# Fused two-block transformer on one core: mixer outputs transposed in steps of their own, and the second layer's transfers moved behind the ninth weights of the first feed-forward

## The chip, the cores and the metric

The kernel runs on one core of a Trainium2 chip. The metric is the device time of one execution in microseconds (us). The program is one launch: TensorE (PE) multiplies, VectorE (DVE) and ScalarE (ACT) read its results and prepare operands, GpSimd (POOL) does a few small operations, and SyncE (SP) issues the transfers from HBM.

## The reference

A first block (retention and RWKV mixers and 16 experts) is followed by a second block of two layers. Only the second block is touched. It works on 256 tokens of 1024 features in fp32:

```
for layer in range(2):
    z = rmsnorm(x, norm_mix[layer]) @ w_in[layer]
    o_a, o_b, o_c, o_d = nsa_mixer(...), diff_mixer(...), mlstm_mixer(...), dilated_mixer(...)
    x = x + concatenate([o_a, o_b, o_c, o_d], axis=-1) @ w_out[layer]
    h = rmsnorm(x, norm_ffn[layer])
    x = x + (silu(h @ w_gate[layer]) * (h @ w_up[layer])) @ w_down[layer]
return rmsnorm(x, norm_final)
```

Each mixer gives 256 of the 1024 columns that `w_out` multiplies. The inner width of the feed-forward is 2816, which the kernel takes in 11 strips of 256.

## The kernel before

**Tiles.** The 256 tokens are two tiles of 128 (index `i`). A matmul of fp32 operands is made of three passes: each operand is split into a rounded part (`hi`, `wh`) and what is left (`lo`, `wl`), and `mm3` adds hi·hi, hi·lo and lo·hi. ACT makes the rounded part of a weight (L346), DVE the rest (L348), in up to four cuts of a tile.

**Weights.** `wsplit` (L351) issues one weight transfer (L354) and the instructions of its split. All weight transfers are issued by SP, which is one queue in order: a transfer that has to wait, for a buffer or for data, holds every later one. There are two buffers `w` for landed weights and three each for `wh` and `wl`, in a pool of the mixers and in another one of the feed-forward.

**Layers.** `stage3` runs `mixers` and then `ffn` for each of two layers; I call the feed-forwards ffn 0 and ffn 1. Between them stand the norms: L2194 loads a row of gains `gn`, L452 and L474 square and scale x, L1671 makes a diagonal matrix `dg` with which TensorE transposes the normed tile, and L1677 and L1678 split it into `b`. In strip f of the feed-forward the weights are `w_gate`, `w_up` and `w_down` (1024 KB each). Strip 0 goes by token tiles (L2131 to L2150), strips 1 to 10 by columns.

**Mixers.** Each mixer is a set of generators ("units") that are advanced in the order of the letters of `STEPS`; a scheduler then orders instructions within the engines. `c` and `d` are projections, `e` to `h` nsa, `i` and `j` diff, `k` and `l` mlstm with `o` and `p` for its end, `m` and `n` the dilated unit of tile 0 and 1. `A` and `B` are `w_out` for mixers 0 and 1, and `z` is `w_out` for mixers 2 and 3 at once. In the dilated unit L1753 makes the probabilities `P`, TensorE transposes them (L395), ACT (L1773) and DVE (L1775) copy them to `PT`, TensorE weighs the values by them, and L1903 normalizes the result.

**The output projection.** `w_out` loads the rows of its mixers and then, for each token tile, transposes the mixer's output (two 128×128 transposes, L395, into a bank of the PSUM ring `pd`), splits it into `oT` (ACT L2106, DVE L2107), multiplies 12 times per bank of 512 columns and adds x (DVE L2116). The ring `pd` has two banks while the mixers run, `pa` has six.

Of the kernel before, what the change touches and what calls it, by code (L numbers as in the profile page):

```python
# [10 lines left out]
F32R = mybir.dt.float32r  # L11
AF = mybir.ActivationFunctionType
OP = mybir.AluOpType
# [3 lines left out]
D = 1024  # L17
T = 256
# [248 lines left out]
class K:  # L267
# [83 lines left out]
    def wsplit(s, src, *shape):  # L351

        w = s.w(*shape)
        s.D.dma_start(w, src)  # L354
        return s.split(w)

    def mm3(s, out, a, b, start=True, stop=True):
# [75 lines left out]
def c128(i):  # L433
    return slice(128 * i, 128 * i + 128)


ALL = slice(None)


def both(w, *ix):  # L440
    return [a[ix] for a in w]
# [21 lines left out]
def normed(k, x, r, g, y):  # L463

    for n in range(2):
        sl = slice(512 * n, 512 * (n + 1))
        k.V.scalar_tensor_tensor(y[:, sl], x[:, sl], r, g[:, sl], op0=OP.mult, op1=OP.mult)


def gained(k, x, g, y):  # L470

    for n in range(2):
        sl = slice(512 * n, 512 * (n + 1))
        k.V.tensor_tensor(y[:, sl], x[:, sl], g[:, sl], op=OP.mult)  # L474
# [1207 lines left out]
def proj_t(k, L, l, m):  # L1682
# [3 lines left out]
    for b in range(2):  # L1686
        for c in range(8):
            k.mm3(p[:, b, :], both(w, ALL, c, c128(b)), both(L.hT, ALL, c), c == 0, c == 7)
    z = k.t([128, 2, 256], "z2", NZ2)
    if m % 2:  # L1690
# [6 lines left out]
def proj_r(k, L, l, n0, n):  # L1697
# [3 lines left out]
    for i in range(2):  # L1701
        p = k.ps("pd")[:, :n]
        for c in range(8):
            k.mm3(p, both(L.hT, ALL, c, c128(i)), both(w[c // 4], ALL, c % 4), c == 0, c == 7)
        r = k.t([128, n], "z2", NZ2)
        if i:
# [17 lines left out]
def rope2(k, u, rot, c, s):  # L1724
# [7 lines left out]
    else:  # L1732
        p = k.ps().rearrange("p (b t) -> p b t", b=2)
        k.mm(p, k.tab(rot), u)
    o = k.t([128, 2, 256], "z2", NZ2)
    t = k.t([128, 2, 256], "q2", 3)
# [347 lines left out]
def add_into(k, acc, x, then):  # L2084

    for i in range(2):
        m = Rms(k)
        for n in range(2):
            sl = slice(512 * n, 512 * (n + 1))
            k.V.tensor_tensor(x[i][:, sl], acc[i][n], x[i][:, sl], op=OP.add)  # L2090
            m.add(x[i][:, sl], n)
        then(i, m)


def w_out(k, l, oc, qs, x, tag, then=None):

    w = [k.wsplit(k.A["w_out_2"][l, q], 2, 1024) for q in qs]
    yield
    for i in range(2):
        o = []  # L2100
        for q in qs:
            p = k.ps("pd")[:, :256].rearrange("p (c t) -> p c t", c=2)
            for c in range(2):
                k.tr(p[:, c], oc[i][:, c128(2 * q + c)])
            hi, lo = [k.t([128, 2, 128], "oT", 4, dt=F32R) for _ in range(2)]
            k.S.activation(hi, p, AF.Copy)  # L2106
            k.V.tensor_tensor(lo, p, hi, op=OP.subtract)  # L2107
            o.append((hi, lo))
        m = then and Rms(k)
        for n in range(2):  # L2110
            sl = slice(512 * n, 512 * n + 512)
            p = k.ps(tag)
            for j in range(len(qs)):
                for c in range(2):
                    k.mm3(p, both(o[j], ALL, c), both(w[j], ALL, c, sl), c == 0 and j == 0, c == 1 and j == len(qs) - 1)
            k.V.tensor_tensor(x[i][:, sl], p, x[i][:, sl], op=OP.add)  # L2116
            if m:
                m.add(x[i][:, sl], n)
        if m:
            then(i, m)  # L2120
        yield


def ffn(k, l, hT):
    V, S, G, A = k.V, k.S, k.G, k.A
    acc = [[k.ps() for n in range(2)] for i in range(2)]
    late = []

    def gate(p, o):

        S.activation(o, p[0], AF.Tanh, scale=0.5)  # L2131
        V.scalar_tensor_tensor(o, o, 1.0, p[0], op0=OP.add, op1=OP.mult)
        V.scalar_tensor_tensor(o, o, 0.5, p[1], op0=OP.mult, op1=OP.mult)

    def by_tiles(w):

        hd = [k.t([128, 2, 256], "hd", 4, dt=F32R) for _ in range(2)]
        for i in range(2):
            p = k.ps("pd").rearrange("p (m n) -> p m n", m=2)
            for m in range(2):  # L2140
                for c in range(8):
                    k.mm3(p[:, m, :], both(hT, ALL, c, c128(i)), both(w[m], ALL, c), c == 0, c == 7)
            th = k.t([128, 256], "q1", NQ1)
            gate([p[:, m, :] for m in range(2)], th)
            p = k.ps("pd")
            for b in range(2):
                k.tr(p[:, c128(b)], th[:, c128(b)])
            for b in range(2):
                S.activation(hd[b][:, 0, c128(i)], p[:, c128(b)], AF.Copy)
                V.tensor_tensor(hd[b][:, 1, c128(i)], p[:, c128(b)], hd[b][:, 0, c128(i)], op=OP.subtract)  # L2150
        return hd

    for f in range(11):
        w = []
        for n in ("w_gate_2", "w_up_2"):
            w.append(k.wsplit(A[n][l, f], 8, 256))
        wd = k.wsplit(A["w_down_2"][l, f], 2, 1024)
        hd = by_tiles(w) if f == 0 else []
        for b in range(2) if f else ():
            p = k.ps("pd").rearrange("p (m t) -> p m t", m=2)  # L2160
            for m in range(2):
                for c in range(8):
                    k.mm3(p[:, m, :], both(w[m], ALL, c, c128(b)), both(hT, ALL, c), c == 0, c == 7)
            th = k.t([128, 256], "q1", NQ1)
            gate([p[:, m] for m in range(2)], th)
            x = k.t([128, 2, 256], "hd", 4, dt=F32R)
            S.activation(x[:, 0], th, AF.Copy)
            V.tensor_tensor(x[:, 1], th, x[:, 0], op=OP.subtract)  # L2168
            hd.append(x)
        late.append((f, hd, wd))  # L2170
        if f == 9:
            continue
        for i in range(2):
            for g, hd, wd in late:
                for b in range(2):
                    for n in range(2):
                        k.mm3(acc[i][n], [hd[b][:, m, c128(i)] for m in range(2)],
                              both(wd, ALL, b, slice(512 * n, 512 * n + 512)), g == 0 and b == 0, g == 10 and b == 1)
        late = []
    return acc  # L2180


def stage3(k, x, y, out):

    rms = k.rms
    with ExitStack() as st, ExitStack() as right:
        k.pool = k.bpool = s3 = k.open(st, "s3")
        w = k.open(right, "s3w", side="right")
        k.tq, k.nb8 = ("q2", 3), 2
        k.flip = False  # L2190

        def norm(name):
            g = k.t([128, 1024], "gn", 2, s3)
            k.D.dma_start(g, k.rowap(name))  # L2194
            if name == "nfin":
                return lambda i, m: normed(k, x[i], m.get(), g, y[i])

            def then(i, m):
                gained(k, x[i], g, y[i])
                rms[i] = m.get()  # L2200

            return then

        for l in range(2):
            with ExitStack() as s1:
                k.banks(s1, "ps4", pa=6, pd=2)
                k.weights(w, 2, 2048, w, 3)
                k.pool = k.open(s1, "s3m")
                mixers(k, l, x, y, rms, norm("nf%d" % l))
            with ExitStack() as s2:  # L2210
                k.banks(s2, "ps5", pa=4, pd=4)
                k.pool = k.open(s2, "s3f")
                k.weights(k.pool, 2, 2048, k.pool, 3)
                hT = norm_t(k, y, rms)
                add_into(k, ffn(k, l, hT), x, norm("nfin" if l else "nm1"))
        for i in range(2):
            for n in range(2):
                sl = slice(512 * n, 512 * (n + 1))
                k.D.dma_start(out[c128(i), sl], y[i][:, sl])
    k.pool = k.base  # L2220


def mixers(k, l, x, oc, rms, then):


    L = Layer()
    L.k2 = [None, None]
    part = lambda r, o, n: [r[i][:, o:o + n] for i in range(2)]
    rope = lambda z, n: rope2(k, z, "rot%d" % n, "c%d" % n, "s%d" % n)

# [56 lines left out]
    def single(f, *a):  # L2287
        f(*a)
        yield

    U = lambda f, *a: f(k, L, *a, oc)
    W = lambda *q: w_out(k, l, oc, q, x, "pd")
    steps = dict(a=first(), b=second(), c=third(), d=fourth(), e=U(nsa_unit, 0, 0), f=U(nsa_unit, 0, 1),
                 g=U(nsa_unit, 1, 0), h=U(nsa_unit, 1, 1), i=U(diff_unit, 0), j=U(diff_unit, 1), k=U(mlstm_unit, 0),
                 l=U(mlstm_unit, 1), m=U(dilated_unit, 0), n=U(dilated_unit, 1), o=single(mlstm_out, k, L, 0, oc),
                 p=single(mlstm_out, k, L, 1, oc), A=W(0), B=W(1), C=W(2), D=W(3),
                 z=w_out(k, l, oc, LAST, x, "pa", then))
    for s in STEPS:
        next(steps[s], None)


NQ1 = 6
LAST = 2, 3
STEPS = "aaaaaaaabhffbbbeebjgihgicjjcicccldkjAdlkidpAdBoBmBAndmnzzz"
NZ2 = 12
NP = 4


# [30 lines left out]
```

## Time and profile before

| | us |
|---|---|
| median of three runs | 1673.66 (1672.74 to 1674.38) |
| the profiled execution | 1671.39 |
| its span | 1669.5 |
| PE busy in the span | 1383.8 (83%) |
| DVE busy | 811.6 (49%) |
| ACT busy | 644.7 (39%) |
| mean granted TensorE clock | 0.918 of full |

The profiled execution is 1.9 us longer than the span in which its instructions lie. The page's chain of waits puts 45% of the span on PE, 25% on transfers (nearly all of it in the experts of the first block) and 14% on DVE. The second block lies in the span's last 750 us. A row of the chain or of the timeline is: start in us, duration in us, engine, line, what it writes and reads, and how many instructions it groups; behind an arrow in square brackets stands the idle time in front of it and what ended that.

### The profile page before, as it was taken

Reading aid. Unit: us, or ns where it says so; the run is one execution under the profiler, and the core shown is the slowest. Engines: PE = TensorE matmul, PEld = TensorE weight load, DVE = VectorE, ACT = ScalarE, POOL = GpSimd, SP = SyncE. Lnnn points to the kernel's source line nnn. Section 1 sums busy time; section 2 is a strip of 40 time slices with the busy share of each in tenths; the row PEclk is TensorE's granted clock in tenths of the full one; section 3 lists DMA queues with packets and bytes.
Section 4 is the critical chain, followed back from the end, with each engine's and each line's share of the span. In section 5 each row is a group of like instructions: output and inputs, shape, how many; then the busy total and the mean of one; then the engine's idle time right before and its main releaser. Section 6 shows DMA issues by size and latency. Waiting matters only on the chain.

```text
span 1669.5 us, 28499 instructions
## 1 busy us (share of the span) xinstructions
PE 1383.8 (83%) x11695; PEld 1052.0 (63%) x11695; DVE 811.6 (49%) x1874; ACT 644.7 (39%) x1527; POOL 241.5 (14%) x311
## 2 busy tenths in 40 slices
PE   6899987878878675656555699889999999899998
PEld 2778865445644332322222387779999988789997
DVE  2455578797541000000000368875556578765564
ACT  3345475754421010100000357554444356444443
POOL 1222344653510000000000111200000022100000
PEclk9999998979879787877877899989999999999999
DMA  9642310703569999999999742355555132345552
GB/s 340 209 150 82 104 51 13 248 13 108 202 276 386 426 427 427 426 426 427 426 427 425 287 163 77 102 214 217 186 193 177 48 132 87 114 152 179 198 177 103
DMA packets 48194, 368.27 MB, mean 221 GB/s; under 512 B 5888, under 2 KB 7552, under 8 KB 23488
## 3 DMA queue, kind: packets, MB, share of 16 engines
q1 hardware_dynamic: 48064, 366.45, 57.2%
q8 instruction: 92, 1.51, 0.4%
q14 instruction: 38, 0.31, 0.1%
HBM read 365.38 MB, written 1.05 MB: 219 GB/s over the span
## 4 chain that ended last, share of the span: by engine, by line
PE 45%; DMA 25%; DVE 14%; ACT 4%; issue 2%; POOL 1%; DVEq 0%; POOLq 0%; SPq 0%; ACTq 0%
PE pd L383 23%; DMA w<-in_w_gu_dram 14%; PE pa L383 12%; DMA w<-in_w_down_dram 9%; PE pm L383 3%; PE c L383 2%; PE pr L383 2%; PE py L383 1%; DVE wl L348 1%; DMA w<-in_w_t_dram 1%; DVE x L825 1%; ACT wh L346 1%; DVE at L844 1%; DVE gs L823 1%; DVE x L2116 1%
## 5 line engine op out<-in xcount | busy, mean ns | idle before, releaser
L348 DVE TENSOR_TENSOR wl<-w,wh 128x512 fp32r<-128x512 f32 (+4 forms) x480 | 306.0, 674 | 147.6 <-ACT wh L346 145.7
L346 ACT ACTIVATE wh<-w 128x512 fp32r<-128x512 f32 (+5 forms) x492 | 263.2, 594 | 169.2 <-PE pa L383 52.6
L383 PE MATMUL pd<-b,wh 128*128 128x256 f32 (+1 forms) x1760 | 319.9, 282 | 0.1
L383 PEld LDWEIGHTS pd<-b,wh 128*128 128x128 f32 (+1 forms) x1760 | 271.1, 187 | 4.6 <-issue 1.1
L383 PE MATMUL pd<-w,b 128*32 128x256 f32 x2048 | 161.5, 472 | 104.9 <-DMA w<-in_w_gu_dram 102.5
L383 PE MATMUL pd<-b,wl 128*128 128x256 f32 (+1 forms) x880 | 247.4, 281 | 1.2 <-DVE wl L348 1.1
L383 PEld LDWEIGHTS pd<-w,b 128*32 128x32 f32 x2048 | 73.6, 130 | 191.1 <-DMA w<-in_w_gu_dram 108.3
L1604 DVE SCALAR_TENSOR_TENSOR th<-th,pd 128x256 f32<-128x256 f32 x16 | 6.7, 421 | 376.1 <-ACT th L1603 376.1
L383 PEld LDWEIGHTS pd<-b,wl 128*128 128x128 f32 (+1 forms) x880 | 164.4, 187 | 3.0 <-DVE wl L348 1.6
L402 POOL TENSOR_TENSOR st<-st,half 128x1 f32<-128x1 f32 (+1 forms) x20 | 17.0, 849 | 845.0 <-DVE st L457 829.1
L383 PE MATMUL pa<-wh,hd 128*128 128x512 f32 x352 | 117.5, 398 | 0.0
L383 PE MATMUL pd<-w,hd 128*32 128x256 f32 x1024 | 87.1, 500 | 26.2 <-DMA w<-in_w_down_dram 20.4
L1603 ACT ACTIVATE th<-pd 128x256 f32<-128x256 f32 x16 | 6.1, 383 | 251.1 <-PE pd L383 251.1
L383 PEld LDWEIGHTS pd<-w,hd 128*32 128x32 f32 x1024 | 39.2, 137 | 68.4 <-DMA w<-in_w_down_dram 24.0
L383 PE MATMUL pd<-wh,b 128*128 128x256 f32 (+2 forms) x320 | 77.4, 328 | 4.2 <-ACT wh L346 3.8
L383 PEld LDWEIGHTS pa<-wh,hd 128*128 128x128 f32 x352 | 64.8, 188 | 16.7 <-DVE hd L2168 3.0
L1624 ACT ACTIVATE ye<-pd 32x256 f32<-32x256 f32 x64 | 24.0, 374 | 126.8 <-PE pd L383 126.2
L383 PE MATMUL pa<-wl,hd 128*128 128x512 f32 x176 | 69.0, 392 | 0.0
L383 PEld LDWEIGHTS pd<-wh,b 128*128 128x128 f32 x320 | 55.2, 196 | 8.5 <-ACT wh L346 4.3
L383 PE MATMUL pd<-wl,b 128*128 128x256 f32 (+2 forms) x160 | 52.4, 328 | 0.6 <-DVE wl L348 0.4
L2131 ACT ACTIVATE q<-pd 128x256 f32<-128x256 f32 x44 | 16.5, 376 | 73.3 <-PE pd L383 73.3
L383 PE MATMUL pm<-hi,wh 128*128 128x256 f32 (+1 forms) x120 | 41.8, 349 | 1.6 <-ACT hi L1236 1.3
(538 smaller groups left out, 2596.2 us busy)
## 6 DMA issues: line engine op xcount, KB each, us to landing
w<-in_w_gu_dram SPq DMA_DIRECT2D x64, 2048.0 KB, 39.2
w<-in_w_down_dram SPq DMA_DIRECT2D x31, 2048.0 KB, 39.2
w<-in_w_down_dram SPq DMA_DIRECT2D x24, 1024.0 KB, 4.9
w<-in_w_gate_dram SPq DMA_DIRECT2D x22, 1024.0 KB, 5.0
w<-in_w_up_dram SPq DMA_DIRECT2D x22, 1024.0 KB, 4.9
w<-in_w_in_dram SPq DMA_DIRECT2D x34, 512.0 KB, 3.7
w<-in_w_mod_dram SPq DMA_DIRECT2D x29, 512.0 KB, 6.5
w<-in_w_t_dram SPq DMA_DIRECT2D x14, 1024.0 KB, 4.8
```

Of the source, the lines that this page charges most:

```text
L346: s.S.activation(out[0][:, c], w[:, c], AF.Copy)
L348: (s.V, s.G)[s.sc % s.every == 0].tensor_tensor(out[1][:, c], w[:, c], out[0][:, c], op=OP.subtract)
L383: s.pe = s.P.matmul(out, lhsT, rhs, start=start, stop=stop, skip_group_check=shared).ins
L402: s.G.tensor_tensor(out, ms, s.half[:, :ms.shape[-1]], op=OP.pow)
L823: F.tensor_tensor(t, M[:, a:b, j:j + 1].to_broadcast(sh), M[:, j:j + 1, :j].to_broadcast(sh), op=OP.mult)
L825: R.marks.append(F.tensor_tensor(M[:, a:b, :j], M[:, a:b, :j], t, op=OP.add).ins)
L844: V.transpose(AT[d][64 + 32 * h:96 + 32 * h].rearrange("p c h t -> p t (c h)")[:, a[h], :], m)
L1603: S.activation(th, pg, AF.Tanh, scale=0.5)
L1604: V.scalar_tensor_tensor(th, th, 1.0, pg, op0=OP.add, op1=OP.mult)
L1624: S.activation(ye[32 * e:32 * e + 32, 256 * j:256 * (j + 1)], p[32 * j:32 * j + 32], AF.Copy)
L2116: k.V.tensor_tensor(x[i][:, sl], p, x[i][:, sl], op=OP.add)
L2131: S.activation(o, p[0], AF.Tanh, scale=0.5)
```

## The change

Three things are changed.

First, `wsplit` remembers its transfer. At strip 8 (the ninth) of a feed-forward the transfer of `w_down` is kept, and the mixers of layer 1 are written under a condition that their transfers on SP come behind it in SP's order. This is an order only; no wait is added.

Second, the transposes of a mixer's outputs leave `w_out`. New steps Q, R, S and T (mixers 0 to 3) transpose both token tiles into banks of `pa`, split them (lines 2104 and 2105 of the new file) and keep the result in a tile of the ring `z2`, which grows from 12 to 14; the ring `oT` is gone.

Third, `w_out` takes both PSUM banks of a token tile at once, runs over the mixers in the outer loop, and adds x (line 2124) when both banks are full. The products, the number of matmuls and of transposes stay.

```diff
-        s.D.dma_start(w, src)
+        s.dma = s.D.dma_start(w, src).ins
...
-def w_out(k, l, oc, qs, x, tag, then=None):
+def o_t(k, L, q, oc):
+
+    L.oT[q] = []
+    for i in range(2):
+        p = k.ps()[:, :256].rearrange("p (c t) -> p c t", c=2)
+        for c in range(2):
+            k.tr(p[:, c], oc[i][:, c128(2 * q + c)])
+        o = k.t([128, 2, 2, 128], "z2", NZ2, dt=F32R)
+        hi, lo = o[:, 0], o[:, 1]
+        k.S.activation(hi, p, AF.Copy)
+        k.V.tensor_tensor(lo, p, hi, op=OP.subtract)
+        L.oT[q].append((hi, lo))
+        yield
+
+
+def w_out(k, L, l, qs, x, tag, then=None):
...
     for i in range(2):
-        o = []
-        for q in qs:
-            p = k.ps("pd")[:, :256].rearrange("p (c t) -> p c t", c=2)
-            for c in range(2):
-                k.tr(p[:, c], oc[i][:, c128(2 * q + c)])
-            hi, lo = [k.t([128, 2, 128], "oT", 4, dt=F32R) for _ in range(2)]
-            k.S.activation(hi, p, AF.Copy)
-            k.V.tensor_tensor(lo, p, hi, op=OP.subtract)
-            o.append((hi, lo))
         m = then and Rms(k)
+        ps = [k.ps(tag) for n in range(2)]
+        for j, q in enumerate(qs):
+            for n in range(2):
+                for c in range(2):
+                    k.mm3(ps[n], both(L.oT[q][i], ALL, c), both(w[j], ALL, c, slice(512 * n, 512 * n + 512)),
+                          c == 0 and j == 0, c == 1 and j == len(qs) - 1)
         for n in range(2):
             sl = slice(512 * n, 512 * n + 512)
-            p = k.ps(tag)
-            for j in range(len(qs)):
-                for c in range(2):
-                    k.mm3(p, both(o[j], ALL, c), both(w[j], ALL, c, sl), c == 0 and j == 0, c == 1 and j == len(qs) - 1)
-            k.V.tensor_tensor(x[i][:, sl], p, x[i][:, sl], op=OP.add)
+            k.V.tensor_tensor(x[i][:, sl], ps[n], x[i][:, sl], op=OP.add)
...
+        if f == 8:
+            k.late = k.dma
...
-                mixers(k, l, x, y, rms, norm("nf%d" % l))
+
+                with k.tc.issue_after(k.late) if l else ExitStack():
+                    mixers(k, l, x, y, rms, norm("nf%d" % l))
...
-STEPS = "aaaaaaaabhffbbbeebjgihgicjjcicccldkjAdlkidpAdBoBmBAndmnzzz"
-NZ2 = 12
+STEPS = "aaaaaaaabhffbbbeebjgihgicjjcicccldQkjAdlkQidpAdRBoRBmSBAnSdmnTTzzz"
+NZ2 = 14
```

SP's queue at the border of layer 0's mixers and ffn 0, before (`w_out`, `gate`, `up` and `down` are of layer 0; `w_r`, `w_t`, `cmp_w` and this `gn` are wanted by layer 1, the `gn` being the gains of its mixers' norm):

```order
L354 DMA w_8660<-in_w_out_dram 128x2048
L354 DMA w_10750<-in_w_r_dram 128x1584
L354 DMA w_10762<-in_w_r_dram 128x1584
L354 DMA w_10828<-in_w_t_dram 128x2048
L2194 DMA gn_10714<-in_row_dram 128x1024
L354 DMA w_8820<-in_w_gate_dram 128x2048
L354 DMA w_8832<-in_w_up_dram 128x2048
L1804 DMA w_10894<-in_cmp_w_dram 128x2048
L354 DMA w_8844<-in_w_down_dram 128x2048
```

and after:

```order
L354 DMA w_8680<-in_w_out_dram 128x2048
L354 DMA w_8812<-in_w_gate_dram 128x2048
L354 DMA w_8824<-in_w_up_dram 128x2048
L354 DMA w_8836<-in_w_down_dram 128x2048
L354 DMA w_8990<-in_w_gate_dram 128x2048
```

The four transfers of layer 1 and its `gn` no longer stand in front of ffn 0's first weights.

They stand now on the same queue in ffn 0's strips 9 and 10; after, from strip 8's `w_down` on:

```order
L354 DMA w_10190<-in_w_down_dram 128x2048
L2204 DMA gn_10706<-in_row_dram 128x1024
L354 DMA w_10334<-in_w_gate_dram 128x2048
L354 DMA w_10742<-in_w_r_dram 128x1584
L354 DMA w_10346<-in_w_up_dram 128x2048
L354 DMA w_10754<-in_w_r_dram 128x1584
L354 DMA w_10820<-in_w_t_dram 128x2048
L354 DMA w_10358<-in_w_down_dram 128x2048
L354 DMA w_10478<-in_w_gate_dram 128x2048
L1804 DMA w_10886<-in_cmp_w_dram 128x2048
L354 DMA w_10490<-in_w_up_dram 128x2048
L354 DMA w_10937<-in_w_t_dram 128x2048
```

They are spread between the weights of the last two strips.

TensorE at the end of layer 1's mixers, between the dilated unit's last projection (`pd` from `b`) and the first matmul of z (`P` are the probabilities, `m` a mixer's output to be transposed, `z,PT` the weighing of the values), before:

```order
L383 MATMUL pd_12256<-wh_12219,b_1431_10717 128x256
L383 MATMUL pa_12283<-z_1714_12254,PT_12289 128x64 x4
L395 MATMUL pa_12297<-tab_1_58,P_12185 128x128 x4
L395 MATMUL pd_12336<-tab_1_58,m_65 128x128 x2
L395 MATMUL pd_12343<-tab_1_58,m_65 128x128 x2
L383 MATMUL pa_12296<-z_1714_12254,PT_12302 128x64
...
L395 MATMUL pa_12308<-tab_1_58,P_12185 128x128 x4
L383 MATMUL pa_12351<-wh_12322,oT_12339 128x512
```

and after:

```order
L383 MATMUL pd_12256<-wh_12219,b_1423_10709 128x256
L395 MATMUL pa_12284<-tab_1_58,P_12115 128x128 x4
L383 MATMUL pa_12283<-z_1706_12254,PT_12289 128x64 x4
L395 MATMUL pa_12297<-tab_1_58,P_12179 128x128 x4
L383 MATMUL pa_12296<-z_1706_12254,PT_12302 128x64
...
L395 MATMUL pa_12308<-tab_1_58,P_12179 128x128 x4
L395 MATMUL pa_12320<-tab_1_58,m_65 128x128 x2
L383 MATMUL pa_12296<-z_1706_12254,PT_12313 128x64
...
L395 MATMUL pa_12326<-tab_1_58,m_65 128x128 x2
L383 MATMUL pa_12349<-wh_12334,z_1685_12138 128x512
```

The first transposes of `P`, which stood among earlier matmuls, have come behind the projection, and both tiles' transposes of the last mixer, and all of the weighing, stand in front of z's first matmul.

## Rows read from the trace of the kernel before

**Rows 1.** Chain of waits, layer 0's end into ffn 0: start, us, what

```profile
1062.10 0.68 DVE z L1739
...
1109.54 0.60 DVE x L2116
...
1111.67 6.64 DMA w<-in_w_gate_dram
1119.80 8.27 PE pd L383 x47
...
1141.32 11.36 PE pd L383 x96
```

**Rows 2.** Chain of waits, the same places of layer 1 into ffn 1

```profile
1419.97 0.68 DVE z L1739
...
1460.69 5.88 PE pa L383 x24
1466.59 0.70 DVE x L2116
...
1473.42 5.82 PE pd L383 x47
...
1492.94 11.36 PE pd L383 x96
```

**Rows 3.** Timeline of SP's queue: start, us issuing, line, what

```profile
1102.14 0.33 SPq L354 DMA_DIRECT2D w<-in_w_t_dram  x1
1111.25 0.33 SPq L2194 DMA_DIRECT2D gn<-in_row_dram  x1
1111.67 0.38 SPq L354 DMA_DIRECT2D w<-in_w_gate_dram  x1
...
1455.18 0.33 SPq L354 DMA_DIRECT2D w<-in_w_up_dram  x1
```

**Rows 4.** Windows: stretch, length, busy PE, PEld, DVE, ACT, POOL, clock, DMA

```profile
1122.00:1124.00 2.00, 2.00 (x11) 2.00 (x11) 1.99 (x4) 1.02 (x2) 0.00 (x0) 0.50 0.72 176
1474.00:1476.00 2.00, 2.00 (x19) 2.00 (x18) 2.00 (x4) 2.00 (x5) 0.00 (x0) 1.00 0.03 8
1426.00:1428.00 2.00, 2.00 (x6) 1.52 (x6) 1.73 (x5) 0.77 (x3) 0.00 (x0) 0.50 0.00 0
```

**Rows 5.** Timeline of PE, end of layer 1's mixers

```profile
1425.36 0.97 PE L383 MATMUL pd<-wh,oT 128*128 128x512 f32 x2 [1.98 <-DVE oT L2107]
...
1449.53 1.00 PE L383 MATMUL pa<-z,PT 128*128 128x64 f32 x8
1450.37 0.61 PE L395 MATMUL pa<-tab,P 128*128 128x128 f32 x4
...
1451.66 1.10 PE L383 MATMUL pa<-z,PT 128*128 128x64 f32 x8
...
1452.96 0.48 PE L383 MATMUL pa<-wh,oT 128*128 128x512 f32 x1
```

**Rows 6.** Chain of waits, the first w_out of layer 1's tail, and the dilated unit's projection

```profile
1425.36 4.16 PE pd L383 x10
...
1440.99 8.71 PE pd L383 x60
```

**Rows 7.** Page, DMA issues: KB each, median us from issue to landing

```profile
w<-in_w_up_dram SPq DMA_DIRECT2D x22, 1024.0 KB, 4.9
```

**Rows 8.** Timeline of ACT, layer 1 into ffn 1, then strips of ffn 0

```profile
1471.94 4.26 ACT L346 ACTIVATE wh<-w 128x512 fp32r<-128x512 f32 x8
...
1260.99 2.01 ACT L346 ACTIVATE wh<-w 128x1024 fp32r<-128x1024 f32 x2 [3.17 <-PE pa L383]
...
1278.01 2.01 ACT L346 ACTIVATE wh<-w 128x1024 fp32r<-128x1024 f32 x2 [3.17 <-PE pa L383]
```

**Rows 9.** Timeline of DVE, the same strip, then a split of w_r

```profile
1279.10 2.36 DVE L348 TENSOR_TENSOR wl<-w,wh 128x1024 fp32r<-128x1024 f32 x2 [3.18 <-ACT wh L346]
...
1098.97 1.52 DVE L348 TENSOR_TENSOR wl<-w,wh 128x396 fp32r<-128x396 f32 x3
```

More of the change, by code (lines that the diff above doesn't have):

```diff
@@ L2226, in mixers @@
     L = Layer()
-    L.k2 = [None, None]
+    L.k2, L.oT = [None, None], {}
     part = lambda r, o, n: [r[i][:, o:o + n] for i in range(2)]
@@ L2291, in mixers @@
     U = lambda f, *a: f(k, L, *a, oc)
-    W = lambda *q: w_out(k, l, oc, q, x, "pd")
+    W = lambda *q: w_out(k, L, l, q, x, "pd")
+    O = lambda q: o_t(k, L, q, oc)
     steps = dict(a=first(), b=second(), c=third(), d=fourth(), e=U(nsa_unit, 0, 0), f=U(nsa_unit, 0, 1),
@@ L2295, in mixers @@
                  l=U(mlstm_unit, 1), m=U(dilated_unit, 0), n=U(dilated_unit, 1), o=single(mlstm_out, k, L, 0, oc),
-                 p=single(mlstm_out, k, L, 1, oc), A=W(0), B=W(1), C=W(2), D=W(3),
-                 z=w_out(k, l, oc, LAST, x, "pa", then))
+                 p=single(mlstm_out, k, L, 1, oc), A=W(0), B=W(1),
+                 z=w_out(k, L, l, LAST, x, "pa", then), Q=O(0), R=O(1), S=O(2), T=O(3))
     for s in STEPS:
```

## The prediction

> **What bounds the kernel now.** I read the chain of waits first, since it says which work sets the end, and compared its two passes through the same code: the end of layer 0's mixers into ffn 0 [rows 1] and the end of layer 1's mixers into ffn 1 [rows 2]. Inside the feed-forwards the chain is TensorE almost without a gap, so only the seams and the mixers can give time. The seams differ. From the same rotation L1739 to the first full strip (the group of 96 matmuls) layer 0 takes 1141.32 − 1062.10 = 79.22 us and layer 1 takes 1492.94 − 1419.97 = 72.97 us. The computation is the same, so layer 0's seam carries 6.25 us of its own. Of these, 5.43 lie behind the last add of x (31.78 against 26.35) and 0.82 before it.
>
> The queue of SP tells why. At layer 0's end the last early transfer, a `w_t` of layer 1, is issued at 1102.14; then the queue stands until `gn` goes at 1111.25, and `gate` follows at 1111.67 [rows 3]. That `gn` is a row of layer 1, and its buffer is free only when the last norm product of layer 0 is done, right behind the last add of x. So ffn 0's first weights stand behind a transfer that waits for the seam itself, and the chain goes through their 6.64 us [rows 1]. In layer 1 nothing of a next layer stands there: `up`, the later of the two, goes at 1455.18, and both are there in time [rows 2, 3]. There is a second cost: while TensorE waits in layer 0 its granted clock falls to 0.50 and is still there at 1122 to 1124, whereas at the same place of layer 1 it is 1.00 [rows 4]; the first group takes 8.27 us for 47 matmuls against 5.82.
>
> **The change, part by part.**
>
> *Transfers behind strip 8's weights.* `w_r` twice, `w_t` and `gn` leave the place ahead of `gate`. Layer 0's seam then has the form that layer 1 has now, and its price is read there, not modelled: −6.25 us, in which the 0.82 are DVE's and ACT's splits of `w_r`, which no longer run between the adds of x. Bounds: at least −5.43, if those splits' room is taken by something else; at most −6.25.
>
> *Where they go.* The three splits and `gn` fall into strips 8 to 10 of ffn 0, `cmp_w` and another `w_t` into strip 10. A strip takes 17.0 us (1278.01 − 1260.99 [rows 8]) and is bound by TensorE; ACT idles 3.17 us in one piece before 1278.01 [rows 8] and DVE 3.18 us before 1279.10 [rows 9]. A cut of `w_r` costs DVE 1.52/3 = 0.51 us [rows 9], a cut of `w_t` 0.6; four cuts of each of three tiles are 6.4 us on DVE and not more on ACT, spread over two strips with over 6 us of such gaps and more in smaller ones. By my walk along the order, `gate`'s split of the next strip becomes ready some 0.6 us later, with over 2 us to spare, and `down` of strip 9 goes out no later than now. Cost zero, hidden by TensorE. Without that cover it is the length of what comes late, up to the 4.9 us of a transfer [rows 7] and more if the queue stands (a rival below). Layer 1's first projections need their splits only after ffn 0, and by the order the queue has passed all of them before strip 10 ends.
>
> *Ffn's first weights, once more.* One wait is new in both layers. With `z2` at 14 and `oT` gone, the buffers of the feed-forward's `w` lie on other tiles than before: `gate` now waits for the last weighing of the dilated unit, and `up` for the very last matmul of z. Queued behind `up` are only later weights of the same feed-forward. In layer 1's times, z ends at about 1466.6; `up` lands 4.9 us later [rows 7], at 1471.5. It is wanted when ACT has split `gate`: ACT starts both at 1471.94 and takes 4.26 for the eight cuts [rows 8], so `up`'s first cut comes at about 1474.1. Slack 2.6 us: cost zero, with the same in layer 0. If it failed by d, the price would be d in each layer.
>
> *The mixers' tail.* All of this counts twice, once per layer; I use layer 1's times. Matmuls and transposes are equal in number, ACT and DVE do the same two operations per transposed pair, so only order counts.
>
> Gain: `A`'s first products now wait for nothing. Before, they stood 1.98 us for DVE's L2107 [rows 5], and the ten behind took 4.16 us [rows 6] at a granted clock of 0.50 [rows 4]; 24 of the same products of z take 5.88 [rows 2], so ten take 2.45. That is up to 1.98 + 1.71 = 3.7 us. But TensorE is not the only one that is late there: the next transposes need diff's norm on DVE, which in DVE's order ends about 1.3 us after the row at 1425.36 whatever TensorE does, and then the dilated unit's rotation, some 3.7 us later still (estimates from that order and the durations of its operations). Following the new order with these durations, the dilated unit's last projection starts at about 1441.8 instead of 1443.9 (1440.99 and 12 products of 0.245 [rows 6]): 2.05 earlier. Its end moves from 1449.53 [rows 5] to 1447.5.
>
> Loss: between that end and z's first product there were 1452.96 − 1449.53 = 3.43 us, filled with weighing. Now tile 0's `P` transposes stand there too (0.46), then a wait for DVE's copy to `PT` behind a weight split (1.5), the weighing of tile 0 (0.84), transposes (0.46), ACT's copy (0.7), half a weighing, transposes and `T`'s first pair (1.1 together), DVE's second copy (0.5), the other half (0.84 with the start), a wait for the normalized output (0.55) and `T`'s second pair (0.23). The waits are the round trip transposes–copy–weighing, 1451.66 − 1450.37 = 1.29 us of which 0.46 are the transposes [rows 5], plus what is queued on DVE. Sum: about 7.6 us, so z starts at 1455.1 and its 48 products, now in one piece, take 11.3 to 11.8. The last add of x comes at 1466.6 to 1466.9, against 1466.59 [rows 2]: what the front gains the tail gives back. I take +0.3 per layer. Bounds: −2.0, if the copies and normalizations hide as they do now and the whole 2.05 is kept; +2.5, if the waits are each one round trip longer or the clock drops as it did at `A`, 1.7 for ten products.
>
> **Sum.** −6.25 + 2 × 0.3 = −5.65 us; the profiled execution of 1671.39 becomes 1665.7, and the median, 2.3 above it, 1668.0.
>
> **The rivals.** *The tail costs more and eats most of the gain.* Each seam of transposes before z leaves TensorE in short bursts for 7.6 us; at `A` a wait of 1.98 was enough for the clock to fall. With +1.5 to +2.5 per layer the sum is −3.25 to −1.25: 1670.4 to 1672.4, no change by the measure of 0.2% or 3.3 us, which is about what a measurement of this kernel can tell from none. For: the round trips are in the order. Against: now, with shorter bursts in the same place, z runs at full rate.
>
> *The clock stays down through z: slower.* At the rate of `A`'s ten, 0.416 us each, against 0.245, a whole z of 48 costs 8.2 us more in each layer: −5.65 + 16.4 = +10.8, 1684.4. It decides from 27 of the 48 products in each layer on (27 × 0.171 × 2 = 9.2, that is 3.6 above the median). For: the stretch ahead of z now holds mostly transposes, small weighings and waits. Against: at `A` the clock was back after ten products. The Trainium skill, "TensorE: Matmul & The Clock Gate", section "Part 4: PE-mode transpose", says that transposes do not count as busy TensorE in the way matmuls do; by that rule the change, which gathers transposes in front of z, would come nearer to this rival. The transposes of this trace, four in 0.61 us [rows 5], are too few to show it either way.
>
> *Ffn 0's strips stall: slower too.* If `w_t` had to wait on SP for a split that ACT takes up only at the end of strip 9, `down` of strip 9 and `gate` of strip 10 behind it would land some 12 us late: about 1675 to 1680. The order puts that split earlier, so it is unlikely.
>
> *The tail keeps its lead.* −2.0 per layer: −10.25, 1663.4. Or *the edge moves the transfers, but `gate` stays late* since something else holds it: then −0.8 at most from the seam, about 1673; the order shows nothing of the kind.
>
> **How the numbers follow.** The forecast (−3.3 to −9) gets 0.61, the tail that keeps its lead 0.07, the tail that eats the gain 0.19, the seam that stays late 0.02, the clock in z 0.07, the stalled strips 0.04. Faster by over 0.2%: 0.68; within: 0.21; slower: 0.11. The range takes in the likely case, the better tail nearly to its end and the costlier tail with 1.5 us for the spread of the medians: 1663.0 to 1674.0. It leaves out the two slow rivals and the rim of the best case.
>
> **What would show it.** Right: the chain has no `gate` transfer in layer 0's seam; `gate` and `up` are issued before or at the last product of z; the clock at ffn 0's start is 1.00; from L1739 to the first 96 matmuls both layers take about 73 us; strips 9 and 10 keep 17.0 us. Wrong: DVE or ACT as releasers of TensorE in strips 9 and 10, `up` as releaser in the feed-forwards' first strip, a granted clock of 0.50 in z, or seams of 75 us and more from the waits in front of z.

## The result

The changed kernel takes 1685.33 us (median of 6 runs, 1683.59 to 1687.13) against 1672.53 of the kernel before (6 runs, 1670.66 to 1674.38). The ratio is 1.0081 with a 95% interval of 1.0071 to 1.0091: about 13 us slower, where I had forecast 5.65 us faster, and outside my range. Its profiled span is 1683.9 us against 1669.5.

I cut the spans of the profiled executions at the same instructions: the first long group of projection matmuls of a mixers' tail (1047.84 before), the last add of x, the first full strip (96 matmuls), the group of 188 matmuls of strips 9 and 10, and the same in layer 1. The add is taken where DVE's timeline has it, in layer 0 before at 1109.46; the chain's row in [rows 1] starts 0.08 later. "e1" and "e8" are two of the experiments below, and e8's execution is the second quickest of twelve.

| stretch, us | before | after | e1 | e8 |
|---|---|---|---|---|
| start to the tail of layer 0 | 1047.84 | 1047.15 | 1047.82 | 1048.12 |
| tail of layer 0's mixers to the last add of x | 61.62 | 68.13 | 61.00 | 61.74 |
| seam into ffn 0, to its first full strip | 31.86 | 27.32 | 25.87 | 26.12 |
| ffn 0, strips 1 to 8 | 136.60 | 140.70 | 138.52 | 138.60 |
| end of ffn 0 and start of layer 1 | 128.73 | 128.61 | 128.75 | 128.42 |
| tail of layer 1's mixers | 59.94 | 67.83 | 60.45 | 61.09 |
| seam into ffn 1 | 26.35 | 27.29 | 27.33 | 26.07 |
| rest | 176.56 | 176.87 | 176.76 | 176.94 |

So the changed kernel gains 4.5 us in layer 0's seam and loses 6.5 and 7.9 in the two tails, 4.1 in ffn 0 and 0.9 in ffn 1's seam.

**The seam.** The chain of waits of the changed kernel, from the last add of x into ffn 0, answers [rows 1]:

```profile
1115.29 0.69 DVE x L2124
...
1122.11 7.34 PE pd L383 x47
...
1142.60 11.36 PE pd L383 x96
```

No transfer of `gate` is left in it. SP's queue [rows 3] shows both weights going out earlier relative to that add: `gate` 13.6 us ahead of it, `up` with it.

```profile
1101.70 0.33 SPq L354 DMA_DIRECT2D w<-in_w_gate_dram  x1
1115.27 0.33 SPq L354 DMA_DIRECT2D w<-in_w_up_dram  x1
```

**The tail.** TensorE's timeline at the end of layer 1's mixers answers [rows 5]; the last matmul of the dilated unit's projection stands right ahead of the first row:

```profile
1454.17 0.60 PE L395 MATMUL pa<-tab,P 128*128 128x128 f32 x4
1456.60 1.66 PE L383 MATMUL pa<-z,PT 128*128 128x64 f32 x8 [1.83 <-DVE PT L1775]
1458.06 1.06 PE L395 MATMUL pa<-tab,P 128*128 128x128 f32 x4
1459.81 1.97 PE L383 MATMUL pa<-z,PT 128*128 128x64 f32 x8 [0.69 <-ACT PT L1773]
...
1466.24 0.78 PE L383 MATMUL pa<-wh,z 128*128 128x512 f32 x1
```

From the first transposes to z's first product it takes 12.07 us. Four transposes, 0.60 at 1454.17, take 1.06 at 1458.06; eight products of the weighing take 1.66 and 1.97 instead of 1.00 and 1.10 [rows 5]. The windows of time show the clock there (stretch, length, busy PE, PEld, DVE, ACT, POOL, granted clock, DMA):

```profile
1452.00:1456.00 4.00, 2.77 (x25) 2.53 (x23) 3.70 (x12) 2.68 (x5) 0.00 (x0) 1.00 0.20 82
1456.00:1460.00 4.00, 2.71 (x13) 2.31 (x14) 2.10 (x3) 0.60 (x1) 0.00 (x0) 0.62 0.00 0
1460.00:1464.00 4.00, 3.65 (x17) 3.24 (x17) 1.12 (x2) 0.38 (x1) 0.00 (x0) 0.50 0.00 0
1464.00:1468.00 4.00, 3.48 (x13) 3.00 (x13) 0.85 (x2) 0.39 (x1) 0.00 (x0) 0.50 0.53 150
1468.00:1472.00 4.00, 4.00 (x13) 3.11 (x12) 0.00 (x0) 0.00 (x0) 0.00 (x0) 0.67 0.27 113
1472.00:1476.00 4.00, 4.00 (x18) 3.20 (x18) 2.97 (x5) 1.45 (x4) 0.10 (x1) 1.00 0.00 0
```

The clock fell to 0.50 (1.2 of 2.4 GHz) after the wait of 1.83 us and was there through the weighing and into z. The same happens in layer 0, where it is at 0.50 from 1096 to 1104. The chain of waits shows what DVE's copy to `PT` stood behind, the split of z's last weight and the transfer of that weight:

```profile
1448.53 4.99 DMA w<-in_w_out_dram
...
1453.63 1.07 ACT wh L346
...
1454.72 1.23 DVE wl L348
1455.94 0.61 DVE PT L1775
```

In layer 0 this transfer takes 5.94 us and the wait of TensorE is 2.78. A second dip of the clock lies ahead of the projection, where `B`'s products stand:

```profile
1432.00:1436.00 4.00, 2.73 (x8) 1.58 (x8) 3.10 (x8) 1.57 (x5) 1.38 (x1) 0.63 0.00 0
1436.00:1440.00 4.00, 3.53 (x14) 2.83 (x15) 3.10 (x10) 0.00 (x0) 1.11 (x1) 0.51 0.20 33
```

There TensorE had waited 1.90 us, for DVE. A wait of this length does not always end so: at the same place of layer 0 TensorE waits 1.91 and 1.86 us (until 1068.55 and 1072.67), and the clock stays at 1.00.

**Ffn 0.** In strip 8 TensorE waits for `hd`, the split of the product that `w_down` multiplies (ACT L2177 and DVE L2178). The first row is of PE's timeline, the next are of ACT's, the last of DVE's:

```profile
1278.66 0.50 PE L383 MATMUL pa<-wh,hd 128*128 128x512 f32 x1 [2.01 <-ACT hd L2177]
```

```profile
1270.96 0.54 ACT L346 ACTIVATE wh<-w 128x396 fp32r<-128x396 f32 x1 [2.79 <-DMA w<-in_w_r_dram]
1271.40 0.40 ACT L2177 ACTIVATE hd<-q 128x256 fp32r<-128x256 f32 x1
1271.71 3.98 ACT L346 ACTIVATE wh<-w 128x396 fp32r<-128x396 f32 x8
...
1278.19 0.42 ACT L2177 ACTIVATE hd<-q 128x256 fp32r<-128x256 f32 x1 [0.26 <-DVE q L2141]
```

```profile
1272.35 4.54 DVE L348 TENSOR_TENSOR wl<-w,wh 128x396 fp32r<-128x396 f32 x8
```

The first cut of `w_r` stands at the head of ACT's queue and waits 2.79 us for its transfer. The feed-forward's own `hd` is queued behind it, and then, on ACT and on DVE, eight cuts stand ahead of the strip's second `hd`, for which TensorE waits. The list of transfers of ffn 0's stretch (KB, us from issue to landing) shows that `w_r` needs 9.4 us to land there, between `gate` and `up`:

```profile
w<-in_w_r_dram SPq DMA_DIRECT2D x2, 792.0 KB, 9.4
```

In the kernel before, ahead of the seam, the same transfers landed in 4.3:

```profile
w<-in_w_r_dram SPq DMA_DIRECT2D x2, 792.0 KB, 4.3
```

### The profile page after: what moved, and what is told of

Same layout as the page of the kernel before. It is cut to its first block, busy times and chain, and to the rows that moved or that the text cites. A ratio compares the mean times of both kernels' runs of the same rounds, so it can differ in the third digit from the quotient of the medians.

```text
span 1683.9 us, 28485 instructions
## 1 busy us (share of the span) xinstructions
PE 1392.5 (83%) x11695; PEld 1063.5 (63%) x11695; DVE 811.2 (48%) x1874; ACT 644.8 (38%) x1527; POOL 244.7 (15%) x311
## 4 chain that ended last, share of the span: by engine, by line
PE 44%; DMA 25%; DVE 12%; ACT 6%; issue 2%; POOL 1%; DVEq 0%; POOLq 0%; ACTq 0%; SPq 0%
PE pd L383 21%; DMA w<-in_w_gu_dram 14%; PE pa L383 12%; DMA w<-in_w_down_dram 9%; PE pm L383 4%; PE c L383 3%; DVE wl L348 2%; PE pr L383 2%; PE py L383 1%; ACT wh L346 1%; DMA w<-in_w_t_dram 1%; PE pa L395 1%; DMA w<-in_w_out_dram 1%; DVE kb L730 1%; ACT P L1753 1%
## 5 line engine op out<-in xcount | busy, mean ns | idle before, releaser
L383 PE MATMUL pd<-w,b 128*32 128x256 f32 x2048 | 157.3, 463 | 105.6 <-DMA w<-in_w_gu_dram 103.2
```

The costliest lines, as they stand in the source:

```text
L383: s.pe = s.P.matmul(out, lhsT, rhs, start=start, stop=stop, skip_group_check=shared).ins
```

## The experiments

**Do the parts add up?** One kernel has the order edge alone, the other the transpose steps and the new `w_out` alone.

```diff
 e1: the kernel before, with
+        s.dma = s.D.dma_start(w, src).ins
+        if f == 8:
+            k.late = k.dma
+                with k.tc.issue_after(k.late) if l else ExitStack():
+                    mixers(k, l, x, y, rms, norm("nf%d" % l))
 e2: the changed kernel, with
-                with k.tc.issue_after(k.late) if l else ExitStack():
+                with ExitStack():
```

> The kernel before with the order edge alone: the second layer's transfers behind strip 8's down weights, w_out as it was. Theory (the parts add up): layer 0's seam gains about 5.4 us and 0.8 us of split work, strips 8 and 9 of ffn 0 lose about 3.7 us as in the changed kernel, both mixers' tails keep the times of before (61.7 and 59.9 us); together 1 to 2.5 us faster than before. Rival (the edge also causes the longer tails): 5 us or more slower than before.

> The changed kernel without the order edge. Theory (the parts add up): both tails keep their 6.4 and 7.9 us, the seam of layer 0 keeps its wait for gate: 14 to 16 us slower than before. Rival (the edge is the cause): within 3 us of before.

The edge alone: 0.9979 (0.9966 to 0.9992) of before, 3.5 us faster. The steps alone: 1.0101 (1.0082 to 1.0121), 17 us slower, a little beyond the 14 to 16 expected. The edge isn't the cause of the tails: with it alone they take 61.00 and 60.45 us, and the steps without it lose 9.0 and 8.1 (70.61 and 68.07). By the ratios the parts add up: −3.5 and +16.9 make +13.4, and the whole is +13.5. The edge does what I had said in the seam, 5.99 us there and 0.62 ahead of it, and costs 1.9 in ffn 0, not the 3.7 expected, so its gain is larger than expected too. Its first full strip in ffn 0 follows the last add of x at 1108.82:

```profile
1134.69 11.36 PE pd L383 x96
```

**Is it the clock?** Now TensorE gets more to do: products that nobody reads, in an unused half of a PSUM bank, where it waits. If the waits themselves were the price, this could only cost time.

```diff
 e5: the changed kernel, in weigh (dilated unit only), behind the transposes of P
+        for _ in range((0, 6 if i else 14)[bool(junk)]):
+            with k.tc.issue_after(tr), k.tc.high_priority(offset=2000):
+                tr = k.P.matmul(po[:, 256:512], junk[:, 0], junk.rearrange("p c t -> p (c t)"), start=True, stop=True, ...).ins
 e6: e5, and in o_t for mixer 1, tile 0, ahead of its transposes
+            for _ in range(16):
+                with k.tc.issue_after(last):
+                    last = k.P.matmul(p[:, 256:], junk[:, 0], ...).ins
```

> The changed kernel with extra products, whose results nobody reads, on TensorE while it waits for the copies of the dilated unit's transposed probabilities: 14 and twice 6 products of 256 columns per layer, some 3 us of work at the full clock. Clock theory (TensorE's waits let the granted clock fall to 0.50, and the weighing and z's first products run at half rate): the clock stays at 1.00 there, and the kernel becomes faster by 3 to 5 us per layer, 6 to 10 in all, though it does more. Rival (the round trips of copies and DVE's queue set the time, the clock is a by-product): same or up to 4 us slower than the changed kernel.

> As the kernel with extra products at the weighing, and 16 more in front of the transposes of mixer 1's output, where TensorE stands 1.9 us in the changed kernel and the clock falls for mixer 1's first products. Clock theory: another 1.5 us per layer, 3 in all, faster than with the products at the weighing alone. Rival: no further gain, or up to 2 us slower.

With 26 more products per layer at the weighing: 1.0025 (1.0010 to 1.0041) of before; with 16 more: 1.0009 (0.9997 to 1.0021). The changed kernel has 1.0081. So doing more work wins 9 us; between the two kernels with extra products the medians differ by 2.5 us and the intervals overlap. TensorE's timeline of the first of them (line 1772 holds the extra products):

```profile
1450.08 0.60 PE L395 MATMUL pa<-tab,P 128*128 128x128 f32 x4
1450.44 1.92 PE L1772 MATMUL pa<-z 128*128 128x256 f32 x14
1452.40 1.10 PE L383 MATMUL pa<-z,PT 128*128 128x64 f32 x8
1453.34 0.61 PE L395 MATMUL pa<-tab,P 128*128 128x128 f32 x4
...
1458.79 0.48 PE L383 MATMUL pa<-wh,z 128*128 128x512 f32 x1
```

and its windows there:

```profile
1452.00:1456.00 4.00, 3.95 (x34) 3.57 (x33) 1.90 (x3) 0.60 (x1) 0.00 (x0) 1.00 0.00 0
1456.00:1460.00 4.00, 3.48 (x25) 3.08 (x24) 1.97 (x4) 0.77 (x2) 0.00 (x0) 1.00 0.26 51
```

The clock stays at 1.00. From the first transposes to z's first product it takes 8.71 us instead of 12.07, and from there to the last add of x 11.52 instead of 13.50; layer 1's tail goes from 67.83 to 62.50. Layer 0's tail gains less, 2.2 us, though the clock stays at 1.00 from 1092 on: there z's weights landed 1.4 us later than in the changed kernel, counted from the tail's start, and the first weighing waits 1.94 us for them even behind the extra products. Not all of the 9 us is this: of the 10.3 us between the two profiled spans 7.5 lie in the tails and 3.5 in ffn 0, where `w_r` lands in 7.5 us and not in 9.4 and the strips take 137.18; the start of the span gives some back.

The 16 products ahead of mixer 1's transposes came out as expected by the number, but their profile doesn't show the expected way. The clock still falls behind them (0.50 at 1076 to 1078 in layer 0, 0.57 at 1430 to 1434 in layer 1). Layer 1's tail is no shorter for them, 62.46 against 62.50. Layer 0's is 2.1 shorter, since z's last weight lands in 4.8 us there and not in 6.8. Whether they gain anything is not shown.

The same runs say what the dip at `B` costs in layer 1. In the first of the two the clock is at 1.00 there all through, in the second it dips, and from the tail's start to the first transposes of `P` they take 42.27 and 42.29 us, the changed kernel 42.26. So that dip isn't what holds the tail; without it the chain runs over the norms on DVE and POOL instead.

**Why does TensorE wait there?** The first probabilities' transposes have come behind the projection. One kernel puts them back, and gives the copies to `PT` the same priority:

```diff
 e8: the changed kernel, in weigh
-                if m:
-                    st.enter_context(k.tc.issue_after(tr))
-                    st.enter_context(k.tc.high_priority(offset=2000))
+                if m:
+                    st.enter_context(k.tc.issue_after(tr))
+                if m or early:
+                    st.enter_context(k.tc.high_priority(offset=early or 2000))
 and the copy to PT likewise; early is 300 for the dilated unit's tile 0, else 0
```

> The changed kernel with the transposes of the dilated unit's first probabilities ahead of its last projection again, as they stood in the kernel before; nothing else moved. Order theory (their round trip behind the projection is part of the loss): the wait of 1.8 us and their own 0.5 go, 2 to 3 us per layer, 4 to 6 us faster than the changed kernel; if the clock then also stays up longer, up to 9. Rival (the two round trips of tile 1 and the clock set the time alone): within 2 us of the changed kernel.

1.0006 (0.9990 to 1.0023): some 12.5 of the 13 us are gone, more than either expectation had. In the profile 2.1 us of the gain lie in ffn 0, where `w_r` lands in 8.8 us; the tails give 13.1. The timeline of TensorE in its profiled execution:

```profile
1440.09 0.60 PE L395 MATMUL pa<-tab,P 128*128 128x128 f32 x4
...
1446.29 1.00 PE L383 MATMUL pa<-z,PT 128*128 128x64 f32 x8
1447.13 0.61 PE L395 MATMUL pa<-tab,P 128*128 128x128 f32 x4
...
1452.57 0.48 PE L383 MATMUL pa<-wh,z 128*128 128x512 f32 x1
```

The first copy to `PT` (on DVE at 1440.94) now stands ahead of the last split of z's weights, and the first weighing follows the projection at once, at the full rate; the tails take 61.74 and 61.09 us. But that execution is the second quickest of twelve that lie between 1666.85 and 1681.16. The mean granted clock of the four quickest is 0.919 to 0.922, of the four slowest 0.910 to 0.915; in which stretch the slow ones lose it, no trace shows. The next kernel asks whether it is the clock that spreads them:

```diff
 e10: e8, with the 16 extra products ahead of mixer 1's transposes, and 6 and 6 at tile 1's weighing
```

> The changed kernel with the first probabilities' transposes ahead of the projection again, and extra products that nobody reads in front of mixer 1's transposes (16) and at tile 1's weighing (6 and 6). Clock theory (the executions with early transposes spread from 1667 to 1681 us because the clock falls in some of them and not in others): the clock stays up in the tail, the median is 4 to 7 us below the 1673 of that kernel, and the spread between executions is under 6 us. Rival (the spread has another cause): the median within 2 us of it, spread of 10 us or more.

0.9983 (0.9974 to 0.9992), 11 runs between 1665.69 and 1670.51: the spread of 14.3 us has become 4.8, and the clock in layer 1's tail is 1.00 in every window of 4 us from 1418 to 1458. In layer 0 it still falls at `B`, to 0.50 at 1074 to 1076. By the ratios the median is 3.8 us below that of e8, just short of the 4 to 7 expected. The clock theory is made likely by this, not shown: the kernel before, run beside each of the two, also spread less beside the second (4.8 us over 15 runs against 9.5 over 28). This is the whole change, mended in two places, and 2.8 us faster than before.

**What does the transfers' new place cost, and must they move?** One kernel moves only `gn`, one sets the edge two strips later.

```diff
 e3: the kernel before, late kept at f == 0, and
+            with k.tc.issue_after(k.late) if name == "nf1" else ExitStack():
+                k.D.dma_start(g, k.rowap(name))
 e4: e1 with
-        if f == 8:
+        if f == 10:
```

> The kernel before with one transfer moved: the gains row gn of the second layer (512 KB, one issue) comes behind the first down weights of ffn 0 on SP; the weight transfers of layer 1 stay where they were. Theory (gn's wait alone holds gate): layer 0's seam from the last add of x to the first full strip goes from 31.8 to 26.4 to 27.3 us, strips 8 and 9 of ffn 0 keep 17.0 us since no weights are split there, 4.5 to 5.5 us faster than before. Rival (w_r and w_t, their transfers and splits, are what delays the seam): within 1.5 us of before.

> The kernel before with the order edge, but behind the down weights of the last strip (f = 10) and not of the ninth. Theory (ffn 0's lost time is the splits of w_r waiting at the head of ACT's queue in strip 8): strips 8 and 9 keep 17.0 us, the seam gains as with the edge at the ninth, 5 to 7 us faster than before, if layer 1's first projection isn't kept waiting. Rival (the transfers then land too late for layer 1): the stretch from ffn 0's last products to layer 1's first mixers grows by 3 us or more, and the gain is under 3 us.

`gn` alone: 0.9979 (0.9968 to 0.9991). The timeline of SP shows `gate` in front of the last add of x (1109.70), right behind a `w_t`, without a wait for `gn`:

```profile
1102.39 0.33 SPq L354 DMA_DIRECT2D w<-in_w_t_dram  x1
1102.81 0.38 SPq L354 DMA_DIRECT2D w<-in_w_gate_dram  x1
```

Ffn 0 keeps its 136.65 us. The seam gains only 2.35 us (29.51) and not 4.5 to 5.5. ACT and DVE still split `w_r` and `w_t` between the norms, and the clock falls there as before:

```profile
1118.00:1122.00 4.00, 3.77 (x16) 3.48 (x17) 4.00 (x8) 3.52 (x7) 0.00 (x0) 0.50 0.07 8
```

The edge behind the last strip: 0.9962 (0.9949 to 0.9975), 6.4 us faster. The strips keep their 17.0 us, but the splits and a `w_t` now come at ffn 0's end: from the first full strip to layer 1's tail it takes 268.95 us instead of 265.33, so that 3.6 us are lost there. Of the expectation both halves came: the stretch grew as the rival had it, and the gain is the theory's. By the profiles it nets about what the edge at the ninth strip nets (1618.5 us from the tail of layer 0 to the end, against 1618.7), though its median is lower; whether it is better, the intervals leave open.

**Can the old tail be helped too?** The kernel before also has a dip, at `A` [rows 4, 6].

```diff
 e7: e3, and in w_out for mixer 0, tile 0, behind the transposes
+            for _ in range(16 if q == 0 and i == 0 else 0):
+                with k.tc.issue_after(last), k.tc.high_priority(offset=2000):
+                    last = k.P.matmul(bank[:, 256:], w[0][0][:, 0, :128], w[0][0][:, 0, :256], start=True, stop=True, ...).ins
 e12: e7, and
+        with k.tc.issue_after(k.late) if l else ExitStack():
+            L.zk = proj_t(k, L, l, 1)
```

> As the kernel with gn alone moved, and 16 extra products of 256 columns, whose results nobody reads, in front of mixer 0's first w_out products, where TensorE of the kernel before stands 2 us and the clock falls to 0.50 for ten products. Clock theory: those products run at the full clock, 1 to 1.7 us less per layer, 2 to 3.4 us faster than with gn alone. Rival (the next waits, on DVE's and POOL's norms and rotations, take it back): within 0.7 us of gn alone.

> w_out as before; the gains row gn and the first transposed weights w_t of layer 1 behind the first down weights of ffn 0, w_r left early; 16 extra products in front of mixer 0's first products. Theory (in the kernel with gn alone, the splits of w_t between the norms still cost the seam 1 to 2 us of its 29.5 or 27.7): the seam falls to about 26.4 us, ffn 0 keeps 136.6, 1 to 1.5 us faster than gn with the extra products (0.9965 of before). Rival (the seam's rest is the granted clock, or the splits move into strip 1 and stall it): within 0.5 us of it or slower.

The extra products at `A`: 0.9965 (0.9952 to 0.9977), against 0.9979 with `gn` alone; the tails take 60.44 and 58.55 us where they took 61.56 and 59.71, 1.1 each, the lower end of what was expected, with the clock at 1.00 all through both. With `w_t` moved too: 0.9960 (0.9946 to 0.9974). From the last add of x to the group of 188 matmuls it is 1.4 us shorter (162.92 against 164.35), but the times don't tell the two kernels apart. The seam, 29.51 with `gn` alone, is 27.65 in the first, in whose profile the clock is at 1.00 there, and 26.42 in the second; so of the 3.2 us that `gn` alone left above layer 1's 26.35, some 1.9 go with the clock and 1.2 with `w_t`'s splits. Both are faster than before and than the changed kernel, by 6 to 7 us and by 19 to 20.

## Why the prediction was wrong

**The bound and the seam: right.** `gate` had been held by `gn`, and without the four transfers layer 0's seam has layer 1's form. I had said −6.25; the edge alone gives −5.99 and −0.62. In the changed kernel 4.5 of it show, its first group of 47 taking 7.34 us and not 5.82 [rows 2]; the clock at ffn 0's start, which I had said would be 1.00, is 0.53 from 1124 to 1126.

**The new waits of `gate` and `up`: right that they are covered.** `up` goes with z's last product, as predicted, and lands in time: no transfer stands in the chain of either seam. Ffn 1's seam is 0.9 longer, but so it is with the edge alone (27.33), where the wait does not exist; what both show is a clock of 0.50 in the first group (1488 to 1490 and, with the edge alone, 1472 to 1474).

**Where the transfers go: wrong.** I took the splits' work (6.4 us on DVE) against the gaps and found room. There was room, but not in order: ACT's queue waits at its head, and DVE's cuts come behind ACT's. The landing time that I had in mind was the 4.9 us of [rows 7]; among `gate` and `up` `w_r` takes 7.5 to 9.4 us. Price 0 predicted, 0.6 to 4.1 us measured, by how late it lands: 0.6 where `w_r` took 7.5 us, 2.0 at 8.8, 4.1 at 9.4. The rival with stalled strips named the wrong holder, SP instead of ACT, and had 0.04.

**The tail: wrong, and this decides.** I had +0.3 per layer with bounds of −2.0 and +2.5; it was +6.5 and +7.9. By steps, in layer 1 (the changed kernel's clock reading runs 5.3 us late there): `A` runs without its wait, as said. The projection was to start at 1441.8 and starts about 1.6 later: of the 2.05 that the front was to gain 0.6 came. That isn't the dip at `B`, since with the extra products at the weighing, where layer 1 has no such dip, it starts no earlier. The rotation on DVE, whose time I had only estimated, ends some 0.8 later than I had it; what makes the other half isn't traced. From the first transposes of `P` to z I wrote 7.6 us, at the durations of [rows 5]; the terms as listed make 7.2, and it took 12.07. Z and its adds were to take 11.3 to 11.8 and took 13.5. The order and the waits were as I had walked them (1.83 for the 1.5 of DVE's copy, 0.69 for 0.7, 0.35 for 0.5, 0.52 for 0.55); in layer 0 the first is 2.78, since z's weight lands later. The term that failed is the duration of everything between them: I priced transposes, weighing and the first products of z at the full clock, and the dip, where I allowed one, at 1.7 for ten products. With extra products the same order takes 8.71 and 11.52, close to the sum, in layer 1; with `P`'s transposes early, another order, the tails are 61.74 and 61.09, which is +0.1 and +1.2. So from the projection on the walk was right, and its unit prices held only while the clock did.

**The rival of the clock: right in kind, wrong in place and price.** I had put it into z, at 27 of 48 products and more to decide, with 0.07. It took the weighing and about ten products of z. Against it I had set that at `A` the clock was back after ten products. So it was in z; what I had left out is that it could fall ahead of z already, through the weighing. Against the costlier tail I had set that z runs at full rate now "with shorter bursts in the same place"; but the round trip behind the projection was new, and behind that wait the clock goes down. The rule on transposes that I had cited from the Trainium skill, "TensorE: Matmul & The Clock Gate", section "Part 4: PE-mode transpose", pointed to this rival. That the transposes are to blame, rather than the waits between them, no run here shows: the extra products fill the one and dilute the other.

## What to carry to other kernels

Where an order gathers short work and round trips on TensorE in front of a long run of products, price the stretch at both clock levels, not at the durations of the order that exists; a test with products that nobody reads can tell which of the two it is, if the profile is read for where the gain came from. A transfer moved into a stretch bound by another engine is not hidden by idle time alone: ask which in-order queue its first consumer joins, and what stands behind it there if the transfer lands late (here 9.4 us among others and 4.3 alone). And when one small transfer holds a queue, try to move that one first.

## What was not expected of the hardware

Extra products made the kernel faster, by 9 us of 1685, and the two tails of the profiled execution shorter by 7.5: with 26 matmuls of 256 columns per layer, 1.92 us for fourteen of them, the clock stayed at 1.00 through a stretch that it had spent at 0.50. And waits of the same length need not end alike: after 1.90 us at `B` the clock fell in layer 1, and after 1.91 and 1.86 us in layer 0 of the same execution it did not.
